# An offline list scheduler's model of the vector, scalar and GpSimd engines gets partition-quadrant gaps, sum gaps and a shared-port rule

## The chip, the cores and the metric

The kernel runs on one core of one Trainium2 chip. The metric is the device time of one execution in microseconds (us). The core's engines are called by the names of the profile: PE (TensorE, matrix products; PEld its weight loads), DVE (VectorE), ACT (ScalarE), POOL (GpSimd) and SP (SyncE, which issues the DMAs). Each engine works through its own list of instructions strictly in the order in which the program wrote them, and waits at semaphores for results of the others.

## The reference

One sequence of 512 tokens, width 1024, float32 throughout. Two layers of mLSTM beside sliding-window attention, with a squared-ReLU MLP; then one block of three attentions (called NSA below):

```python
for l in range(2):
    h = rmsnorm(x, norm_mix_g[l])
    proj = h @ w_in[l]                    # mLSTM q,k,v,o and gates; attention q,k,v; two branch gates
    hm = mlstm(silu(causal_conv(mqk)), mv, igate, fgate)          # 4 heads
    hm = headnorm(hm) * g * sigmoid(mo)
    ha = sliding_window_attention(aq, ak, av, sinks, rel_bias)    # 16 heads, window 128
    x = x + (sigmoid(ga) * (hm @ w_branch_m) + sigmoid(gb) * (ha @ w_branch_a)) @ w_out[l]
    h = rmsnorm(x, norm_mlp_g[l])
    x = x + square(relu(h @ w_up[l])) @ w_down[l]                 # 1024 -> 4096 -> 1024
x = rmsnorm(x, final_norm_g)
q, kv, g, z = split(rms_norm(x, gain) @ w_in2)
kc, vc = compress_kv(k_c), compress_kv(v_c)      # blocks of 32 keys, stride 16, a small MLP
o = sigmoid(g) * [attend(q,kc,vc), attend_selected(q,k_s,v_s), attend_window(q,k_w,v_w)] * silu(z)
out = x + o.sum(branches) @ w_out2
```

With 512 tokens the selected blocks are all blocks, so that branch is full causal attention.

## The kernel before

Every large product is a `gemm` of 128x128 stationary tiles with 128x512 moving tiles. Both operands are split into a high and a low part of a shorter float format, and `mm3` adds three products (high x high, high x low, low x high). Weights come from memory in tiles `raw` of 128x1024 or less; ACT writes their high part `wh`, and DVE or POOL their low part `wl` (`raw` minus `wh`). `xgh` and `xgl` are the two parts of the normalised activations. PSUM results of gemms are tiles `g` (four buffers, the same four also hold `gt`, the token-major products); attention scores are `S`, transposed probabilities `PT`, their parts `ph` and `pl`, head outputs `O`. In the attention, DVE adds bias and takes a maximum (`L`, `mn`), ACT takes the exponential with its row sum (`L`, `den`), `rd` is the reciprocal of the sum, ACT and DVE scale `L` by it, PE transposes it into `PT`, ACT and DVE split that, and PE multiplies by `v`. In the mLSTM part, `sums` and `bc` are small matmuls for norms and broadcasts, `ST` the products with the state. `cf` and `Z` belong to the compression of keys in NSA: `cf` is a scaled gemm result, and 32 small DVE operations `Z<-cf` write the overlapping blocks with the position added.

Nothing is issued while the program is built. The class `Recorder` takes each operation with its operands, works out which earlier operations it has to wait for, and `issue(RESERVE, WINDOW)` then runs a list scheduler over the whole program: it keeps a clock for each engine, always takes the operation that can start first by its model (for ties the one that is earliest in the program), at most 500 operations ahead of the oldest one not yet done, and hands out buffers. On PE, `pick` prefers an operation whose weights are loaded by the time the previous matmul ends. When all is ordered, one loop calls `op.fn(*op.args, **op.kw)`, so every instruction of the trace carries the same line (L320 before the change). The times in the model decide the order and nothing else.

The model before: `cost` gives the length of each operation; `LAT` the delay from an end on one engine to a start on another; `OVERLAP` a fixed amount by which the next operation of ACT, DVE or POOL starts ahead of the end of the last (100, 78, 38 ns); an operation with an `accum_out` (a sum along with its result) costs ACT 190 ns and DVE 150 ns more. `port` marks DVE operations with two inputs from SBUF, and POOL's: while one engine's such operation runs, the other engine's are not chosen, and an operation without the mark goes ahead of them.

## Time and profile before

| quantity | value |
| --- | --- |
| time of three runs | median 2189.2 us (2188.83 to 2190.84) |
| the profiled execution's own time | 2191.76 us |
| its span, first to last instruction | 2190.0 us |
| mean granted TensorE clock | 0.997 of full speed |
| PE busy | 2143.8 us, 98% of the span |
| DVE busy | 1383.5 us, 63% |
| ACT busy | 1065.0 us, 49% |
| POOL busy | 444.2 us, 20% |

The profile is of one execution; its time lies 1.76 us above its span, which is what starting and ending take outside the first and last instruction, and 2.6 us above the median of the three runs. "Busy" counts the time in which an engine has an instruction under way; the matmul ends are modelled, so a busy PE shows that it waits for nobody, not that each matmul is as fast as can be.

### The profile page before, as it was taken

The page shows a single profiled execution, that of the slowest core. Times are in us where ns is not written, and L with a number is a line of the kernel's source. Part 1 is how long each engine was busy: PE and PEld are TensorE (multiplying, and loading weights), DVE is VectorE, ACT ScalarE, POOL GpSimd, SP SyncE. Part 2 cuts the span into 40 slices and gives each one's busy share as a digit, 9 for nine tenths or more (in the row PEclk, how much of TensorE's full clock was granted, in tenths as well). Part 3 has the DMA queues.
Part 4 walks back from the last instruction along what each step waited for, and adds up shares of the span by engine and source line. Part 5 has one row for each costly group of instructions (what it writes and reads, how often), then busy time and mean ns, then how long its engine had stood idle before and what let it go on. Part 6 is the DMA issues. An engine that isn't in the chain of part 4 may idle for free.

```text
span 2190.0 us, 28079 instructions
## 1 busy us (share of the span) xinstructions
PE 2143.8 (98%) x10389; PEld 1773.4 (81%) x10389; DVE 1383.5 (63%) x2591; ACT 1065.0 (49%) x2066; POOL 444.2 (20%) x502
## 2 busy tenths in 40 slices
PE   8999999999999999999999999999999899999988
PEld 6787788888888888887777888888888798888777
DVE  7688995444343445678897445434435777888786
ACT  4466773234232334456675223323324356787783
POOL 2133551002000002014454002000001604232211
PEclk9999999999999999999999999999999999999999
DMA  5223222433333333322322333333333253222221
GB/s 159 81 66 90 81 73 88 134 96 95 98 96 96 97 97 116 97 78 76 97 68 77 120 111 97 96 96 97 97 100 116 85 167 97 68 65 67 92 93 43
DMA packets 72426, 206.10 MB, mean 94 GB/s; under 512 B 9761, under 2 KB 18593, under 8 KB 72289
## 3 DMA queue, kind: packets, MB, share of 16 engines
q1 hardware_dynamic: 72288, 204.31, 30.3%
q8 instruction: 81, 1.33, 0.2%
q14 instruction: 57, 0.46, 0.1%
HBM read 197.86 MB, written 6.42 MB: 93 GB/s over the span
## 4 chain that ended last, share of the span: by engine, by line
PE 43%; DVE 6%; ACT 2%; issue 2%; POOL 1%; POOLq 0%; DVEq 0%; ACTq 0%
PE g L320 34%; PE O L320 2%; PE PT L320 2%; PE S L320 2%; PE go L320 2%; DVE L L320 1%; PE gt L320 1%; DVE hal L320 1%; DVE wl L320 1%; PE hid L320 1%; POOL vb L320 0%; DVE Z L320 0%; ACT L L320 0%; DVE q L320 0%; ACT wh L320 0%
## 5 line engine op out<-in xcount | busy, mean ns | idle before, releaser
L320 ACT ACTIVATE wh<-raw 128x1024 fp32r<-128x1024 f32 (+2 forms) x344 | 355.5, 1034 | 784.6 <-PE g L320 590.8
L320 PE MATMUL g<-xgl,wh 128*128 128x512 f32 x1512 | 596.1, 394 | 2.5 <-DVE xgl L320 2.5
L320 PE MATMUL g<-xgh,wl 128*128 128x512 f32 x1512 | 594.8, 393 | 3.3 <-POOL wl L320 3.3
L320 PE MATMUL g<-xgh,wh 128*128 128x512 f32 x1512 | 595.4, 394 | 1.7 <-ACT xgh L320 1.5
L320 DVE TENSOR_TENSOR wl<-raw,wh 128x1024 fp32r<-128x1024 f32 (+2 forms) x327 | 410.9, 1257 | 125.4 <-ACT wh L320 124.4
L320 PEld LDWEIGHTS g<-xgh,wl 128*128 128x128 f32 x1512 | 284.9, 188 | 60.1 <-POOL wl L320 5.0
L320 PEld LDWEIGHTS g<-xgl,wh 128*128 128x128 f32 x1512 | 284.7, 188 | 59.7 <-DVE xgl L320 5.0
L320 PEld LDWEIGHTS g<-xgh,wh 128*128 128x128 f32 x1512 | 285.1, 189 | 56.5 <-ACT xgh L320 2.2
L320 POOL TENSOR_TENSOR sq<-sq 128x512 f32<-128x512 f32 x50 | 80.5, 1609 | 596.1 <-ACT sq L320 586.3
L320 PE MATMUL g<-hidh,wh 128*128 128x512 f32 x512 | 199.2, 389 | 0.0
L320 PE MATMUL g<-hidh,wl 128*128 128x512 f32 x512 | 199.2, 389 | 0.0
L320 PE MATMUL g<-hidl,wh 128*128 128x512 f32 x512 | 199.2, 389 | 0.0
L320 DVE TENSOR_TENSOR x<-x,g 128x512 f32<-128x512 f32 x80 | 55.0, 687 | 204.5 <-PE g L320 204.5
L320 ACT ACTIVATE L<-L,mn 128x256 f32<-128x256 f32 (+3 forms) x256 | 131.4, 514 | 38.8 <-DVE mn L320 35.7
L320 DVE SCALAR_TENSOR_TENSOR hz<-g,Rb 128x512 f32<-128x512 f32 x64 | 44.3, 692 | 157.8 <-PE g L320 152.3
L320 PEld LDWEIGHTS g<-hidh,wl 128*128 128x128 f32 x512 | 96.1, 188 | 20.0
L320 PEld LDWEIGHTS g<-hidh,wh 128*128 128x128 f32 x512 | 96.1, 188 | 20.0
L320 PEld LDWEIGHTS g<-hidl,wh 128*128 128x128 f32 x512 | 96.1, 188 | 19.8
L320 DVE TENSOR_TENSOR pl<-PT,ph 128x512 fp32r<-128x512 f32 (+1 forms) x160 | 79.8, 526 | 27.8 <-ACT ph L320 26.4
L320 PE MATMUL gt<-wh,xgh 128*128 128x512 f32 (+3 forms) x256 | 88.5, 347 | 5.0 <-DVE cf L320 5.0
L320 PE MATMUL gt<-wl,xgh 128*128 128x512 f32 (+3 forms) x256 | 88.5, 347 | 2.2 <-DVE wl L320 2.2
L320 PE MATMUL gt<-wh,xgl 128*128 128x512 f32 (+3 forms) x256 | 88.6, 346 | 0.0
(308 smaller groups left out, 3734.2 us busy)
## 6 DMA issues: line engine op xcount, KB each, us to landing
raw<-wf SPq DMA_DIRECT2D x258, 512.0 KB, 3.5
raw<-wn SPq DMA_DIRECT2D x41, 512.0 KB, 3.8
raw<-wmv SPq DMA_DIRECT2D x16, 512.0 KB, 3.6
x<-x SPq DMA_DIRECT2D x16, 256.0 KB, 4.2
bt<-E SPq DMA_DIRECT2D x16, 256.0 KB, 5.0
xsp<-x SPq DMA_DIRECT2D x16, 256.0 KB, 2.0
raw<-w SPq DMA_DIRECT2D x8, 512.0 KB, 3.8
bn<-E SPq DMA_DIRECT2D x16, 256.0 KB, 4.3
```

The source lines that it names most:

```text
L320: op.fn(*op.args, **op.kw)
```

## The change

No operation is added, removed or resized; each engine has the same instructions before and after, in another order. The diff replaces the numbers and a rule in the scheduler's model:

```diff
-OVERLAP = {PE: 0, ACT: 100, DVE: 78, POOL: 38, SP: 0}
+GAP = {ACT: (-95, 24, -2, 116), DVE: (-82, 31, -75, 40), POOL: (-38, 43, -38, 43)}
+ACC = {ACT: 93, DVE: 9}
+PORT = {DVE: 143, POOL: 116}
...
-            return 200 + 0.84 * n - (22 if _psum(ins[0]) else 0) + 88 * min(scalars, 2), False
+            return 192 + 0.842 * n - (22 if _psum(wide[0]) else 0) + 88 * min(scalars, 2), False
...
+            if name == "tensor_tensor_scan":
+                return 1209, both
+            if name in ("tensor_copy", "tensor_scalar") and not _psum(wide[0]):
+                return 150 + n / 1.92 + 60 * scalars, n > 4
+            return 148 + 1.05 * n + 60 * scalars, both
...
-            op.occ += 100 if eng == ACT else 60
-            op.cost += 190 if eng == ACT else 150
...
+        def gap(op):
+            e = op.eng
+            if e not in GAP:
+                return 0.0
+            held = wq[e].get(op.writes[0], op.writes[1]) != op.writes[1] or \
+                any(rq[e].get(m, x) != x for m, x in op.reads)
+            return GAP[e][2 * after[e] + held]
...
-                held = max(f, port[DVE if e == POOL else POOL]) if e in (DVE, POOL) else f
-                for k, s in ((0, f), (1, held)):
-                    if ready[e][k]:
-                        c = (s, ready[e][k][0], e, k)
-                        if best is None or c[0] < best[0] or c[0] == best[0] and c[2] == best[2] and c[1] < best[1]:
-                            best = c
...
+                lim = f + (GAP[e][0] if e in GAP else 0)
+                while pending[e] and pending[e][0][0] <= lim:
+                    heappush(ready[e], heappop(pending[e])[1])
+                if ready[e]:
+                    s = lim
+                elif pending[e]:
+                    s = pending[e][0][0]
...
-                op.start, op.end = t, t + op.cost
-                free[e] = t + op.occ
-                if op.port:
-                    port[e] = op.end - 60
+                t = max(t, free[e] + gap(op))
+                op.start, f = t, t + op.cost
+                if op.port:
+                    h = hold[POOL if e == DVE else DVE]
+                    if h > t:
+                        f = max(f, h + op.cost - PORT[e])
+                    hold[e] = f
+                free[e], after[e] = f, op.acc
+                op.end = f + (ACC[e] if op.acc else 0)
```

How far the order moves: of PE's instructions two thirds keep their place, of DVE's and ACT's about half; the furthest on PE goes 79 places, on DVE 36, on ACT 20, on POOL 5, on SP 3. The MLPs and the products with `w_branch` and `w_out` (about 360 to 840 us and 1200 to 1700 us of the trace) are unmoved. Three places follow.

**The start, DVE.** `sq` are squares for the norm, `xgl` the low parts of the activations, `oh` one-hot tables for the bias, `wl_151` the low part of the weight that the first token-major product `gt` needs. Before:

```order
SCALAR_TENSOR_TENSOR xgl_97<-x_95,pc_74,xgh_96 128x512
TENSOR_TENSOR sq_112<-x_98 128x512
SCALAR_TENSOR_TENSOR xgl_100<-x_98,pc_74,xgh_99 128x512
...
CAST oh_174<-oh_173 64x512
CAST oh_179<-oh_178 64x512
CAST oh_183<-oh_182 64x512
TENSOR_TENSOR selh_125<-ident_115 36x512
TENSOR_TENSOR wl_151<-raw_149,wh_150 128x528
```

After:

```order
SCALAR_TENSOR_TENSOR xgl_97<-x_95,pc_74,xgh_96 128x512
SCALAR_TENSOR_TENSOR xgl_100<-x_98,pc_74,xgh_99 128x512
...
TENSOR_TENSOR sq_112<-x_98 128x512
...
TENSOR_TENSOR wl_151<-raw_149,wh_150 128x528
TENSOR_TENSOR wl_154<-raw_152,wh_153 128x528
TENSOR_TENSOR wl_157<-raw_155,wh_156 128x528
...
CAST oh_174<-oh_173 64x512
```

The four casts `oh` go behind `wl_151`, `wl_154` and `wl_157`, and `sq_112` behind the last `xgl`.

**Attention of layer 1, near 253 us, PE.** `g_673` is a gemm that ends there, `g_711` the next one, `PT` and `O` the attention of one group of heads. Before:

```order
MATMUL g_673<-xgl_106,wh_671 128x512
MATMUL PT_648<-ident_115,L_636 128x128 x2
MATMUL PT_651<-ident_115,L_638 128x128 x2
MATMUL g_711<-xgh_81,wh_709 128x512
MATMUL g_711<-xgh_81,wl_710 128x512
MATMUL g_711<-xgl_82,wh_709 128x512
MATMUL g_711<-xgh_87,wh_709 128x512
MATMUL O_647<-ph_649,v_138 128x256
```

After:

```order
MATMUL g_673<-xgl_106,wh_671 128x512
MATMUL g_711<-xgh_81,wh_709 128x512
...
MATMUL g_711<-xgl_91,wh_709 128x512
MATMUL PT_648<-ident_115,L_636 128x128 x2
MATMUL PT_651<-ident_115,L_638 128x128 x2
MATMUL g_711<-xgh_93,wh_709 128x512
MATMUL g_711<-xgh_93,wl_710 128x512
MATMUL g_711<-xgl_94,wh_709 128x512
MATMUL O_647<-ph_649,v_138 128x256
```

Nine matmuls of `g_711` now stand ahead of the first `PT`.

**The start of NSA, near 1736 to 1754 us, DVE.** `cf_2886` and `cf_2891` empty the two PSUM buffers that the products `gt` still lack; `wl_2905` is the low part of the weight that these products read next. Before (23 more `Z` between the fourth row and the fifth, 8 behind the last):

```order
TENSOR_TENSOR cf_2872<-g_2876,Rb_2855 128x512
TENSOR_TENSOR cf_2877<-g_2881,Rb_2855 128x512
TENSOR_TENSOR cf_2886<-g_2890,Rb_2855 128x512
TENSOR_TENSOR Z_2868<-cf_2872,pc_74 64x4x31
...
TENSOR_TENSOR cf_2891<-g_2895,Rb_2855 128x512
TENSOR_TENSOR wl_2905<-raw_2903,wh_2904 128x608
```

After (15 more `Z` behind the third row, 15 more behind the sixth):

```order
TENSOR_TENSOR cf_2872<-g_2876,Rb_2855 128x512
TENSOR_TENSOR cf_2877<-g_2881,Rb_2855 128x512
TENSOR_TENSOR Z_2868<-cf_2872,pc_74 64x4x31
...
TENSOR_TENSOR cf_2886<-g_2890,Rb_2855 128x512
TENSOR_TENSOR cf_2891<-g_2895,Rb_2855 128x512
TENSOR_TENSOR Z_2882<-cf_2886,pc_74 64x4x31
...
TENSOR_TENSOR wl_2905<-raw_2903,wh_2904 128x608
```

`cf_2891` has 16 `Z` ahead of it instead of 24, and `wl_2905` all 32 instead of 24. On PE the four tiles of `gt` were filled side by side before; now the first two go on through their next weight tiles before the other two begin, and the four matmuls that read `wl_2905` first come behind 16 others that wait for `cf_2886` and `cf_2891`. Before, the wait for `cf_2891` had 26 matmuls up to and with the last of these four behind it.

## Rows read from the trace of the kernel before

**Rows 1.** The page, section 1: busy time of each engine.

```profile
PE 2143.8 (98%) x10389; PEld 1773.4 (81%) x10389; DVE 1383.5 (63%) x2591; ACT 1065.0 (49%) x2066; POOL 444.2 (20%) x502
```

**Rows 2.** Stretches: length, busy us (instructions) of PE, PEld, DVE, ACT, POOL; clock; DMA.

```profile
0.00:60.00 60.00, 51.46 (x241) 39.52 (x242) 43.20 (x80) 28.28 (x47) 14.47 (x22) 0.97 0.49 153
60.00:360.00 300.00, 292.13 (x1467) 238.19 (x1465) 246.25 (x547) 188.12 (x436) 112.53 (x134) 1.00 0.26 77
360.00:900.00 540.00, 540.00 (x2435) 448.25 (x2434) 249.85 (x290) 178.67 (x230) 35.48 (x24) 1.00 0.34 105
900.00:1200.00 300.00, 292.18 (x1468) 238.06 (x1467) 244.35 (x552) 187.52 (x435) 111.30 (x133) 1.00 0.26 78
...
1680.00:1800.00 120.00, 113.75 (x595) 97.44 (x594) 86.89 (x127) 62.15 (x97) 45.16 (x60) 0.99 0.39 125
1800.00:2040.00 240.00, 239.47 (x1346) 203.67 (x1344) 193.44 (x497) 176.52 (x414) 75.15 (x86) 1.00 0.27 81
2040.00:2190.00 150.00, 134.86 (x726) 111.18 (x726) 111.41 (x276) 92.55 (x222) 26.70 (x28) 0.97 0.22 71
```

**Rows 3.** PE's waits over the whole span: total us, times, longest us.

```profile
PE PT L320 <- ACT L L320: 11.2, 15, 1.8
PE gt L320 <- DVE cf L320: 5.0, 1, 5.0
PE g L320 <- POOL wl L320: 3.3, 4, 1.3
PE gt L320 <- DVE wl L320: 2.2, 1, 2.2
PE sums L320 <- ACT sqh L320: 2.1, 3, 1.2
PE ST L320 <- DVE w L320: 2.1, 2, 1.0
PE ptc L320 <- DVE Lc L320: 1.9, 1, 1.9
```

**Rows 4.** DVE, timeline at the start: start, us, operation, idle before.

```profile
17.04 1.77 DVE L320 TENSOR_TENSOR sq<-x 128x512 f32<-128x512 f32 x1
...
23.62 2.17 DVE L320 CAST oh<-oh 64x512 fp32r<-64x512 f32 x3
...
26.32 0.69 DVE L320 TENSOR_TENSOR wl<-raw,wh 128x528 fp32r<-128x528 f32 x1
```

**Rows 5.** POOL, timeline at the start.

```profile
14.90 3.36 POOL L320 TENSOR_TENSOR sq<-sq 128x512 f32<-128x512 f32 x2 [1.29 <-ACT sq L320]
```

**Rows 6.** PE, timeline near 250 us.

```profile
249.68 0.39 PE L320 MATMUL g<-xgh,wl 128*128 128x512 f32 x1
...
252.63 0.39 PE L320 MATMUL g<-xgl,wh 128*128 128x512 f32 x1
253.99 0.73 PE L320 MATMUL PT<-ident,L 128*128 128x128 f32 x4 [0.98 <-ACT L L320]
```

**Rows 7.** PE's waits from 240 to 360 us.

```profile
PE PT L320 <- ACT L L320: 4.3, 6, 1.0
```

**Rows 8.** PE's waits from 1080 to 1200 us.

```profile
PE PT L320 <- ACT L L320: 4.7, 7, 1.0
```

**Rows 9.** DVE, timeline of the start of NSA.

```profile
1735.38 1.29 DVE L320 TENSOR_TENSOR cf<-g,Rb 128x512 f32<-128x512 f32 x2 [1.44 <-ACT Rb L320]
...
1737.44 10.42 DVE L320 TENSOR_TENSOR Z<-cf,pc 64x124 f32<-64x124 f32 x24
```

**Rows 10.** PE, timeline of the start of NSA.

```profile
1748.64 0.52 PE L320 MATMUL gt<-wh,xgh 128*128 128x304 f32 x1 [5.02 <-DVE cf L320]
...
1752.23 0.30 PE L320 MATMUL gt<-wh,xgh 128*128 128x304 f32 x1
...
1753.74 0.30 PE L320 MATMUL gt<-wl,xgh 128*128 128x304 f32 x1
```

**Rows 11.** A stretch behind that wait, columns as in rows 2.

```profile
1749.00:1752.00 3.00, 3.00 (x14) 3.00 (x14) 2.99 (x7) 0.00 (x0) 2.94 (x7) 0.50 0.56 173
```

## The prediction

> **What bounds the kernel now.** I read the busy times first: PE is busy for 2143.8 of 2190.0 us [rows 1]. The next engine, DVE, has 63%. So no engine but PE is full, and the change, which adds and removes nothing, can only act through the 46 us in which PE stands still. The table by stretches says where they lie [rows 2]: 8.5 us in the first 60; 7.9 and 7.8 in the mLSTM and attention of the two layers (60 to 360 and 900 to 1200 us); 6.2 at the start of NSA; 0.5 from 1800 to 2040; 15.1 from 2040 on, of which a part follows the last matmul. In 360 to 900 PE is busy for the whole 540.00 us; there the order is unmoved, and nothing can come or go. The list of PE's waits says for whom [rows 3]: transposes `PT` for ACT's scaled `L` 11.2 us, `gt` for one `cf` 5.0, gemms for a POOL-made `wl` 3.3, `gt` for `wl` at the start 2.2, and three of about 2 us. This is the stock from which any gain comes; the gemm itself costs 0.227 us for each matmul (13 steps from 249.68 to 252.63) [rows 6] and stays.

> The sums below are made against the profiled execution's own 2191.8 us; the median of the runs is 2.6 us lower, and I take that off at the end.

> **Start.** DVE works without a pause up to `wl_151`, for which PE waits 2.2 us [rows 3]. Three casts `oh` of together 2.17 us stand right ahead of it and its `selh` [rows 4] and go behind; their results are first read by PE in the bias products, behind all of these `gt`, in the new order too. So `wl_151` comes about 2.1 us sooner, and with it everything behind: **-2.1**. `sq_112` also moves. It took 1.77 us, while a comparable operation alone takes 0.69, because it met POOL's additions, 14.90 to 18.26 us [rows 4, 5]. Bounds: -3.2 if it no longer meets them (1.1 more), -1.0 if another operation meets them in its place. Waits ahead of this one (for `xgl`) are in series with `wl_151` and not counted again.

> **Attention of the two layers.** PE waits 4.3 us in six places and 4.7 in seven for `L` [rows 7, 8], 0.7 us each. At the place shown the wait is 0.98 [rows 6]; the new order puts nine gemm matmuls there, 9 x 0.227 = 2.0 us of work that is ready. Elsewhere I count 5 to 10 such matmuls, late in the phase more. The gemm runs out of matmuls no earlier in sum, since the same ones were done later; what may come back is a wait at the last `O`, whose results the branch product needs, but the next gemms still lie between. I take 80% of 9.0: **-7.2**. Bounds: all (-9.0), or -2.0 where ACT, which is idle ahead of its own scaling as well, makes `L` late by as much again.

> **mLSTM.** Two waits `ST` for DVE's `w`, together 2.1 us [rows 3]: the operation `nMd` that the exponential ahead of `w` reads moves ahead of two splits `kl` on DVE. I take **-2.0** (bounds -2.1 and 0). Against it, the first `sums` matmul stands 17 places earlier on PE, that is 17 x 0.227 = 3.9 us, while the ACT operation `sqh` that it waits for stands only 3 to 10 places earlier; that wait is about 0.5 us now in each layer (`sums`: 2.1 us in three, the longest 1.2 in NSA) [rows 3], and I let each grow by 0.5: **+1.0** (bounds 0 and +2.4, when `sqh` gains 2.6 of the 3.9). `bc` goes five places back, 1.1 us of cover for a wait of 0.4 in each layer: **-0.7** (0 to -0.8).

> **Start of NSA.** Here the change puts a new wait in the place of one that it removes. 24 `Z` take 10.42 us, 0.434 each [rows 9]. Before: PE waits 5.0 us for `cf_2891`, goes on at 1748.64, and starts the first four matmuls that read `wl_2905` until 1753.74, the 26th from there [rows 10]. After: the first two `cf` end near 1737.1 (1735.38 + 1.29, and some 0.5 later, since the norm's `sums` and `bc` move back), 16 `Z` at 0.434 to 1744.1, two `cf` (1.29) to 1745.4, 16 `Z` to 1752.3, `wl_2905` (0.7 as `wl_151` [rows 4]) near 1753.1. PE waits about 2 us for the `cf`, does 16 matmuls, and waits again some 5 for `wl_2905`; of the 26 only four are left then, the last at 1753.1 + 3 x 0.14 = 1753.5. [...] So -0.2 + 1.5: **+1.3**. Bounds -0.2 (no slow stretch) and +1.6. Behind it, `wl_2918` comes later by eight `zl` that DVE does first; they fill pauses of DVE ahead of it, so I take nothing, with the bound +1 inside the range.

> **NSA from 1800 us.** Up to 2040 there is half a microsecond to gain [rows 2]. The attention moves forward by 9 to 27 places on PE against the gemms; DVE's reciprocal and ACT's scaling move forward as well, so that I expect few waits: **+1.0** (0 to +5). From 2040 on lie most of the 3.3 us of waits for POOL's `wl` and the 1.9 for `Lc` (`ptc`) [rows 3]; in the new order attention matmuls stand where the first `wl` is late, and the scores that `Lc` is made from come some ten matmuls (2.3 us) earlier, with two more DVE operations of 0.7 in their way. I take **-3.0** (bounds -7 and +3). DMA issues move by at most three places on SP, and no wait of PE in rows 3 ends with a DMA; nothing for these.

> **Sum.** -2.1 - 7.2 - 2.0 + 1.0 - 0.7 + 1.3 + 1.0 - 3.0 = -11.7; 2191.8 - 11.7 = 2180.1 for a profiled run, and 2177.5 for the median.

> **A rule that speaks against the change.** `sq_112` took 1.77 us beside POOL, and its end, 18.81, lies 0.55 behind that of POOL's additions, 18.26 [rows 4, 5]: it seems to have stood until the port came free. [...]

> **Rivals.** *The waits only move* (within 0.2%, that is 4.4 us): the layers' attention gives the low bound, -2.0, and `sums` takes +2.4, while start, `ST` and `bc` (-4.8), NSA's +1.3 and +5 and no gain at the end follow: +1.9, 2191 us. For it: 0.7 us is short, and the same engines feed the next matmul. Against it: nine ready matmuls for 0.98 us is twice what is missing. I let it stand for all sums from -4.4 to +4.4, at its middle 2189. *DVE stands in POOL's holds* (slower): the model no longer keeps such operations apart. POOL has 134 operations in each layer's stretch [rows 2]; an operation that meets one loses about 1.1 us (1.77 against 0.69) [rows 4]. If 17 more in each layer do, DVE is 37 us later in sum; if half of that reaches PE, which waits for DVE's results in order, that is +18, and 2191.8 - 11.7 + 18 - 2.6 = 2195.5. It decides from about 30 such meetings on; below 20 it is hidden. For it: DVE is busy for 246 of 300 us there. Against it: such meetings happen in the present order too, for the old rule only looked at a port taken when it chose. *More is recovered*: all of the first bounds together, -3.2 - 9.0 - 2.1 - 0.8 - 0.2 - 7 = -22.3, 2167 us.

> **How the numbers follow.** The forecast of some -6 to -17 us has 0.58, more than that 0.10, the waits that only move 0.18, the port 0.14. So faster by over 0.2% (under 2184.8) has 0.68, same 0.18, slower 0.14. 0.2% is about what a measurement of this kernel can tell from no change. The range from 2167 to 2191 leaves out the port and little more; it takes in the waits that only move. The forecast's own range is 2172 to 2183.

> **What the profile after would show.** Right: `PT` for `L` falls from 11.2 to 3 us or less, `ST` for `w` is gone, `gt` for `wl` at the start is followed by the same matmuls 2 us sooner, and near 1750 there are two waits of PE, of about 2 and 5 us, the second on `wl`, with a granted clock of 0.5 behind it. Both layers' stretches are 4 to 5 us shorter. Wrong: many DVE operations of 1.8 us where 0.7 was, with PE waiting for DVE; `sums` or `sc` waits over 1.5 us in a layer; PE waits in NSA between 1800 and 2040.

## The result and the profile after

The changed kernel takes 2165.06 us (median of four runs, 2163.57 to 2165.97), the kernel before, run beside it, 2189.93 (2188.83 to 2190.84): 24.9 us less, a ratio of 0.9886 with a 95% interval of 0.9869 to 0.9903. I had forecast 2177.5, some 12 us less, and a range down to 2167. The sign was right, the size is twice the forecast, and the result lies 2 us below the range. The profiled execution took 2164.52 us with a span of 2162.7, 27.3 below the span of before.

The page of the kernel after, busy times:

```profile
PE 2134.9 (99%) x10389; PEld 1780.6 (82%) x10389; DVE 1375.4 (64%) x2591; ACT 1063.7 (49%) x2066; POOL 439.9 (20%) x502
```

Against [rows 1] PE is busy for 8.9 us less with the same instructions, and it stands idle for 27.8 us in place of 46.2, 18.4 less; together these are the 27.3. That busy time can fall says that "busy" is no fixed amount of work. The stretches after, with the columns of [rows 2]:

```profile
0.00:60.00 60.00, 52.78 (x246) 41.37 (x247) 40.93 (x81) 29.00 (x48) 16.43 (x22) 0.97 0.50 156
60.00:360.00 300.00, 300.00 (x1519) 249.80 (x1518) 246.22 (x552) 190.59 (x439) 108.76 (x134) 1.00 0.28 82
...
900.00:1200.00 300.00, 300.00 (x1516) 250.22 (x1516) 244.27 (x547) 189.75 (x437) 110.04 (x135) 1.00 0.28 82
...
1680.00:1800.00 120.00, 111.22 (x627) 97.40 (x625) 83.97 (x146) 56.29 (x91) 47.54 (x87) 0.97 0.40 121
1800.00:2040.00 240.00, 238.85 (x1345) 204.54 (x1344) 203.92 (x520) 188.90 (x447) 70.05 (x59) 1.00 0.26 77
```

From 60 to 360 us PE's busy time rose from 292.1 to the full 300.0 us, 7.9 more; but the matmuls in brackets rose from 1467 to 1519. At 0.227 us a matmul, 52 more are 11.8 us of work. Read the count beside the time: it is the count that the end follows. PE's waits over the whole span after, columns as in [rows 3]:

```profile
PE gt L346 <- DVE wl L346: 6.3, 1, 6.3
PE sums L346 <- ACT sqh L346: 3.9, 1, 3.9
PE warm L346 <- ACT z L346: 2.3, 1, 2.3
PE gt L346 <- DVE cf L346: 2.3, 1, 2.3
PE g L346 <- POOL wl L346: 2.0, 2, 1.6
PE O L346 <- DVE pl L346: 1.2, 3, 0.8
```

`PT` for `L` (11.2 us before) and `ST` for `w` (2.1) are gone; between 60 and 1200 us the list has no wait of PE at all. Two long ones are new: `sums` at the start, `gt` for `wl` at the start of NSA.

For this kernel and those below I cut the span at the start of certain matmuls that stand at the same work in every order (such as the first `gt_208` that reads `wl_223`, or the first `g_619` that reads `wl_618`). Lengths in us of the profiled executions, up to the last matmul:

| kernel | start | mLSTM 1 | attention + MLP 1 | mLSTM 2 | attention + MLP 2 | start of NSA | rest of NSA |
| --- | --- | --- | --- | --- | --- | --- | --- |
| before | 66.5 | 163.2 | 676.8 | 165.1 | 651.1 | 39.6 | 421.3 |
| after | 65.4 | 159.2 | 668.3 | 161.2 | 642.5 | 41.8 | 417.6 |
| old port rule | 64.1 | 161.5 | 668.8 | 162.9 | 643.4 | 39.9 | 425.7 |
| no quadrant gap | 63.3 | 160.2 | 676.2 | 162.2 | 650.4 | 41.3 | 418.1 |
| none on DVE | 63.9 | 160.2 | 675.9 | 162.2 | 650.0 | 41.9 | 416.7 |
| none on ACT | 64.7 | 159.0 | 670.4 | 161.4 | 644.1 | 42.0 | 418.3 |
| old price of sums | 63.9 | 159.1 | 668.4 | 161.0 | 642.7 | 41.8 | 431.1 |
| older latencies | 65.3 | 159.2 | 668.4 | 161.2 | 642.6 | 42.0 | 414.2 |
| before + quadrant gap | 65.5 | 161.3 | 669.1 | 163.2 | 643.4 | 39.4 | 424.5 |
| last version | 63.9 | 159.2 | 668.4 | 161.2 | 642.6 | 32.8 | 417.7 |

Of the 27.3 us, 17.0 come from the attention of the two layers (8.4 and 8.6), 7.8 from their mLSTM, 1.1 from the start and 3.6 from the rest of NSA; the start of NSA lost 2.2. These differences are of unrounded lengths, and a tenth can differ from the table's.

### The profile page after: what moved, and what is told of

Same layout as the page of the kernel before. It is cut to its first block, busy times and chain, and to the rows that moved or that the text cites. A ratio compares the mean times of both kernels' runs of the same rounds, so it can differ in the third digit from the quotient of the medians.

```text
span 2162.7 us, 28087 instructions
## 1 busy us (share of the span) xinstructions
PE 2134.9 (99%) x10389; PEld 1780.6 (82%) x10389; DVE 1375.4 (64%) x2591; ACT 1063.7 (49%) x2066; POOL 439.9 (20%) x502
## 4 chain that ended last, share of the span: by engine, by line
PE 95%; DVE 2%; POOL 1%; issue 1%; ACT 1%; DMA 0%; SPq 0%; DVEq 0%; POOLq 0%; ACTq 0%
PE g L346 75%; PE gt L346 6%; PE S L346 3%; PE O L346 3%; PE PT L346 2%; PE num L346 1%; PE go L346 1%; PE ST L346 1%; DVE Z L346 1%; POOL vb L346 0%; PE bc L346 0%; PE hid L346 0%; POOL sq L346 0%; PE sums L346 0%; DMA x<-x 0%
## 5 line engine op out<-in xcount | busy, mean ns | idle before, releaser
L346 DVE TENSOR_TENSOR pl<-PT,ph 128x512 fp32r<-128x512 f32 (+1 forms) x160 | 78.9, 525 | 23.3 <-ACT ph L346 22.5
```

## The experiments

Each result is the median of the runs with the lowest and the highest, and then the ratio to the kernel before, run beside it, with its 95% interval in square brackets. Code is shown in extracts; `...` stands for what is left out.

### What each part of the model carries

**Port rule undone.** The changed kernel, but an operation that uses the port is again held back while the other engine has it, and the marks are the old ones.

```diff
-                if ready[e]:
-                    s = lim
...
+                held = max(lim, hold[DVE if e == POOL else POOL] - 60) if e in (DVE, POOL) else lim
+                for k, s in ((False, lim), (True, held)):
+                    mine = [j for j in ready[e] if ops[j].port == k]
...
```

> The changed model with the old port rule: port operations of DVE and POOL are kept apart again, all else new. If the port rule is what freed PE from its waits in the two layers, each layer's stretch gets its 7.5 us of idle back and the time goes to about 2180 to 2190 us. If the gaps and the sums did it, the time stays within 5 us of the changed kernel's 2165. At the start the squares are then kept away from POOL's additions as before, so the wait of 3.9 us for the norm's sums goes and one for a weight's low part of about 2 us comes back, in either case.

Measured 2174.70 us (2173.51 to 2175.63), 0.9929 [0.9906, 0.9951] of before, 9.6 above the changed kernel, which lies between my two forecasts. The attention stays within 0.9 us of the kernel after; the mLSTM gives back 2.3 and 1.7 us of its 4.0 and 3.9, NSA 8.1 behind its start, while the start and the start of NSA are 1.3 and 1.9 shorter. At the start the wait for `sums` is gone and one of 2.2 us for `wl` is back, as expected. The model's port rule, which I feared, is a gain in the mLSTM; what it is worth in NSA the control below leaves open.

**Quadrant gap undone**, on all engines.

```diff
-            return GAP[e][2 * after[e] + held]
+            return GAP[e][2 * after[e]]
```

> The changed model without the gap at a change of partition quadrant: every next operation starts early, as in the old model; sums, port and costs stay new. If the quadrant gap (0.11 us on DVE, 0.12 on ACT, at most some 60 operations in an attention step) carries the gain, PE's waits for the transposes come back and the time goes above 2175 us. If not, it stays at 2160 to 2170.

Measured 2182.21 (2180.05 to 2182.92), 0.9963 [0.9947, 0.9979], 17.1 above the changed kernel. Both layers' attention is back at the length of before, the mLSTM gives back 1.0 each. A line of PE's waits over the whole span of this kernel:

```profile
PE PT L346 <- ACT L L346: 4.7, 10, 1.2
```

Only 4.7 us of these waits are back, 3.5 of them (nine) in the layers, where the waits of all kinds come to 6.7; the two attention stretches are 15.8 us longer than after. A stretch can lose far more than its waits show; I come to that below.

**Price of sums undone.**

```diff
-GAP = {ACT: (-95, 24, -2, 116), DVE: (-82, 31, -75, 40), POOL: (-38, 43, -38, 43)}
-ACC = {ACT: 93, DVE: 9}
+GAP = {ACT: (-95, 24, 5, 124), DVE: (-82, 31, -22, 91), POOL: (-38, 43, -38, 43)}
+ACC = {ACT: 190, DVE: 150}
```

> The changed model with the old price of a sum: its result 190 ns (ACT) or 150 ns (DVE) late instead of 93 and 9, and the engine held as long as before. The exponentials and maxima of the attention all make sums. If that price put the attention in the wrong place, PE waits for the transposes again and the time goes above 2175 us; if not, 2160 to 2170.

Measured 2177.83 (2176.34 to 2178.83), 0.9943 [0.9921, 0.9966], 12.8 above the changed kernel. The time is above the 2175 that I named, but not for the reason that I gave with it: the layers don't change and have no wait for the transposes. The rest of NSA is 13.4 us longer, the start 1.5 shorter.

Undone one at a time, the three parts cost 9.6, 17.1 and 12.8 us, together 39.5, more than the 24.9 of the whole change: they can't be added up.

**A control: the older latencies alone.** The change also replaces four values of `LAT`, the delays between engines, by 1 or 2 ns, which the list of the change does not name; this run puts the old ones back.

```diff
-LAT = {(PE, ACT): 204, (PE, DVE): 200, (PE, POOL): 240, (ACT, PE): 53, (ACT, ACT): 32, (ACT, DVE): 33, (ACT, POOL): 78,
-       (ACT, SP): 26, (DVE, PE): 55, (DVE, ACT): 34, (DVE, DVE): 34, (DVE, POOL): 80, (DVE, SP): 28, (POOL, PE): 54,
+LAT = {(PE, ACT): 202, (PE, DVE): 200, (PE, POOL): 240, (ACT, PE): 53, (ACT, ACT): 32, (ACT, DVE): 33, (ACT, POOL): 79,
+       (ACT, SP): 27, (DVE, PE): 55, (DVE, ACT): 34, (DVE, DVE): 34, (DVE, POOL): 79, (DVE, SP): 28, (POOL, PE): 54,
```

> A control: only the table of delays between engines is the old one, four numbers that differ by 1 or 2 ns; 7% of PE's instructions change places. What an arbitrary small reshuffle is worth: 2162 to 2168 us, with the two layers' stretches still free of waits. If it moves by more than 5 us, single runs of the other three say little about their rule.

Measured 2161.87 (2161.25 to 2162.49), 0.9874 [0.9845, 0.9902]: 3.2 us below the changed kernel, all of it in the rest of NSA, the layers equal to 0.1 us. So in NSA a change of 2 ns that means nothing shuffles the order and is worth 3 us; differences of that size there say nothing about a rule.

**Quadrant gap undone on DVE alone**, and then **on ACT alone**.

```diff
-            return GAP[e][2 * after[e] + held]
+            return GAP[e][2 * after[e] + (held and e != DVE)]
```

> The changed kernel, with the quadrant gap switched off in the model of DVE alone. With the gap off everywhere the attention stretches of the two layers had grown from 113.0 and 119.2 us to 120.9 and 127.1. Theory A (what is mispriced is DVE's work on scores and masks, whose pieces change quadrant from one to the next): attention stretches of 118 to 121 and 124 to 127 us, transposes waiting for L again, 2178 to 2184 us. Theory B (it is ACT's row of exponentials and scalings of L): attention stretches stay within 1.5 us of 113 and 119, and the time within 2160 to 2170. Both in part: 115 to 118 and 121 to 124.

> The changed kernel, with the quadrant gap switched off in the model of ACT alone. Theory A (DVE's gap carries the attention gain): stretches stay within 1.5 us of 113 and 119, 2160 to 2170 us. Theory B (ACT's does): stretches of 118 to 121 and 124 to 127 us, transposes waiting for L some 4.7 us in each layer, 2176 to 2184 us. I hold B the likelier, since the wait that vanished was one for ACT's L.

Without it on DVE 2179.81 (2179.07 to 2180.86), 0.9957 [0.9941, 0.9973]; on ACT 2167.93 (2167.62 to 2168.23), 0.9902 [0.9882, 0.9922]. Theory A holds, but for ACT's stretch in layer 1, which I had allowed 1.5 us: without DVE's gap the attention of the layers loses 7.6 and 7.5 us, without ACT's 2.0 and 1.5, without any 7.9 and 7.8. I had held B the likelier, because the wait that went was one for ACT's `L`: the engine named in that wait was the last in a chain, and by these losses most of the delay came from the engine ahead of it.

**The quadrant gap alone, added to the kernel before.**

```diff
+        more = {ACT: 119, DVE: 113, POOL: 81}
...
+                if wq[e].get(op.writes[0], op.writes[1]) != op.writes[1] or any(rq[e].get(m, x) != x for m, x in op.reads):
+                    t = max(t, free[e] + more.get(e, 0))
...
```

> The kernel before, its model kept, with one thing added: a gap in front of an operation that changes quadrant (ACT 119 ns, DVE 113 ns, POOL 81 ns more). Theory (the quadrant gap alone carries the attention gain): attention stretches fall from 121.1 and 127.5 us to 113 to 115 and 119 to 121, those of the mLSTM stay near 163 and 165, and the time is 2170 to 2176 us. Rival (the gap helps only along with the new prices of sums and of the port, since the old overlaps are wrong in other places too): attention stretches 118 or more and 124 or more, 2182 to 2192 us.

Measured 2174.93 (2174.87 to 2174.98), 0.9934 [0.9914, 0.9954], 14.5 below the kernel before. The theory holds in the time and in the attention: with the MLP it is 7.7 us shorter in each layer (the cut at its end lies 2 us earlier, so the attention alone reads as 111.4 and 117.7). The mLSTM, which I expected unchanged, is 1.8 and 1.9 shorter. The gap alone in the mLSTM and the port rule there (2.3 and 1.7) together come near its 4.0 and 3.9.

The timeline of DVE in the kernel after, inside the attention, shows the two gaps themselves:

```profile
257.62 0.41 DVE L346 TENSOR_TENSOR hal<-O,hah 64x256 fp32r<-64x256 f32 x1
257.96 0.47 DVE L346 CUSTOM_DVE_ANT_0 L<-S,bt,nsink 128x256 f32<-128x256 f32 x1
258.36 0.08 DVE L346 DVE_READ_ACCUMULATOR2_ANT mn<- 128x1 f32 x1
258.46 0.42 DVE L346 TENSOR_TENSOR hal<-O,hal 64x256 fp32r<-64x256 f32 x1
258.92 0.48 DVE L346 CUSTOM_DVE_ANT_0 L<-S,bt,nsink 128x256 f32<-128x256 f32 x1
```

The first `L` starts 0.07 us ahead of the end of the `hal` before it (257.62 + 0.41 = 258.03); the second, behind another `hal` of 64 partitions, 0.04 behind its end (258.46 + 0.42 = 258.88). In the attention of layer 1 before, the trace has some 100 gaps of DVE of the second kind, +0.034 on the mean, and some 130 of the first, -0.08 (reads of an accumulator left out of these). Some 70 of the 100 stand behind an operation without a sum. The old model gave these -0.078, so by this count its DVE ran 70 x 0.113 = 7.9 us ahead of the chip over that stretch; behind a sum, where it let the engine go 0.06 later, it was off by about half as much. That it therefore put PE's `PT` where the model's `L` was ready and the chip's was not is my reading; the runs show that the gap moves the attention's time. They switched the gap in the model, and did not vary the partitions by themselves.

### What a wait costs

**Six, and then twelve, small copies on ACT ahead of 32 scalings of `L`** in the two layers, with the order of the changed kernel otherwise kept: extra work that makes `L` late.

```diff
+            if id(op) in slow:
+                for _ in range(6):
+                    self.scalar.real.activation(self.scr[0], self.scr[1], AF.Copy)
...
```

> The changed kernel with six extra copies of 128x112 on ACT (about 0.2 us each, 1.2 in all, into a tile that nothing reads) ahead of the scaling of L in each of the 32 half steps of the layers' attention; the order is untouched. It shows the cover that the changed order has: with more than 1.2 us of it the layers' stretches stay as they are and the time stays within 3 us; with less, waits of PE for L appear.

> The same with twelve copies, about 2.4 us. PE has to wait in many places now. If a wait costs PE just the idle time that the list of waits shows, the layers' stretches grow by that idle time. If it costs more, because the matmul behind it can't overlap the tail of the one ahead and the next comes late too, they grow by about 0.25 to 0.3 us more for each wait; with some 30 waits that is 8 to 9 us on top.

With six 2216.13 us (2216.12 to 2216.15), 1.0118 of before; with twelve 2300.63 (2299.21 to 2302.04), 1.0504. PE's waits over the whole span with six:

```profile
PE O L351 <- ACT ph L351: 20.1, 17, 1.6
PE PT L351 <- ACT L L351: 19.3, 18, 1.5
```

A copy took 0.29 us, six of them 1.8 where I had 1.2, and the order does not cover that in 35 places. The kernel lost 2216.1 - 2165.1 = 51.1 us and shows 39.4 us of such waits: on the mean each cost its idle time and 0.33 us more, with the late starts that show no idle time counted in. With twelve it lost 135.6 for 88.6 us of waits (34 of them), 1.4 more each; there the mean granted clock also fell (0.969 over the span in place of 0.994 with six, and 0.92 from 60 to 370 us), so that this run can't price the wait alone.

Where such a surplus comes from can be read at one place, where it is 0.27. In [rows 6] the last gemm before the wait starts at 252.63 and `PT` at 253.99. What follows there in the kernel before (timeline of PE):

```profile
254.48 0.48 PE L320 MATMUL g<-xgh,wh 128*128 128x512 f32 x1
254.79 0.40 PE L320 MATMUL g<-xgh,wl 128*128 128x512 f32 x1
```

And the same three steps in the kernel after, where nothing is waited for:

```profile
248.49 0.40 PE L346 MATMUL g<-xgl,wh 128*128 128x512 f32 x1
248.72 0.60 PE L346 MATMUL PT<-ident,L 128*128 128x128 f32 x4
249.08 0.47 PE L346 MATMUL g<-xgh,wh 128*128 128x512 f32 x1
249.40 0.39 PE L346 MATMUL g<-xgh,wl 128*128 128x512 f32 x1
```

Before: 254.79 - 252.63 = 2.16 us; after: 249.40 - 248.49 = 0.91. The wait shown as 0.98 cost 1.25, 0.27 more. A gemm matmul counts as busy for 0.39 us though the next starts 0.227 behind it; of a late start the first 0.16 us lie under that tail and are not shown as idle, and the step behind the wait is 0.13 longer (0.49 against 0.36). The 0.39 is a modelled end, and so the 0.16 (0.39 less 0.227) is an estimate; the starts are measured.

This can be counted for a whole stretch, as start-to-start steps beyond the usual one (the median step of the same two shapes in the kernels before and after, 60 to 1690 us). In the attention of layer 1 before, 12 steps are late by over 0.1 us, 7.2 us in all (8 of them show as waits, 5.3 us); after, none. Without the quadrant gap 23 are, 6.4 us in all, of which the stretch shows 3.0 as idle. Many short late starts weigh like a few long ones and hardly show. With all steps that are late by over 0.02 us, the two attentions come to 20.4 us before and 4.1 after, the two mLSTM to 13.4 and 6.2. The difference, 23.5 us, is nearly all of what the layers gained (24.8), and the trace of before shows only 15.1 us of idle time in these four stretches.

### The two new waits

**Both moved by hand**: the norm's `sums` at the start behind `gt` matmuls that are ready, and `wl_2905` right behind `cf_2891` on DVE; then the same with the older latencies.

```diff
+        w = next(op for op in dve if self.name(op).startswith("wl_2905"))
+        dve.remove(w)
+        n = [i for i, op in enumerate(dve) if self.name(op).startswith("cf_2891")][-1]
+        dve.insert(n + 1, w)
...
```

> The changed order with two places moved by hand, all else in its place. On DVE wl_2905 goes right behind cf_2891, ahead of 16 Z; on PE the norm's sums, sc and bc at the start go behind those products gt that are ready. The first should take away the wait of 6.3 us for wl_2905 and the slow matmuls behind it, 6 to 8 us in all; the second the wait of 3.9 us for the sums, and slow matmuls behind it, 3 to 5 us. Together 2152 to 2157 us. If what follows only waits for Rb (start) or for the 16 Z and the compression (NSA) in its turn, most of it comes back later.

> The control with the old table of delays (2161.9 us) and the same two places moved by hand. If the two moves are worth what the waits cost and nothing else depends on them, it is as much faster than 2161.9 as the kernel without the old table is than 2165: 2149 to 2154 us.

Measured 2159.56 (2159.26 to 2160.85), 0.9861 [0.9846, 0.9876], and 2157.30 (2156.27 to 2158.79), 0.9852 [0.9835, 0.9868], both some 3 us slower than the ranges that I gave. In the first kernel the start gains 1.4 us, the start of NSA 1.9; there the wait of 6.3 became one of 4.4, for `wl_2908`, the next weight, which still stood behind 16 `Z`:

```profile
PE gt L347 <- DVE wl L347: 4.4, 1, 4.4
```

**The last version**: as the second of these, and at the start of NSA `cf_2886` behind 8 `Z`, `cf_2891` behind 14, `wl_2905` and `wl_2908` behind the first 16, `wl_2911` behind five more; DVE's later `zl` and ACT's `zh`, parts of the operands of `hid`, were moved along with these.

```diff
+        n = find(dve, "cf_2877", True) + 1
+        dve[n + 8:n + 8] = c86
+        dve[n + 15:n + 15] = c91
+        dve[n + 18:n + 18] = w5 + w8
+        dve[n + 25:n + 25] = w11
...
```

> The changed kernel with the older table of latencies between engines (2161.9 us measured), the norm's sums at the start behind gt matmuls that are ready, and at the start of NSA on DVE and ACT cf_2886 behind 8 Z, cf_2891 behind 14, the weights wl_2905 and wl_2908 behind the first 16 Z, wl_2911 behind 5 more. Theory (the wait for wl there is one of order alone): PE's waits of gt for wl go, one for cf of 1 to 2 us stays, the stretch at the start of NSA falls from 41.8 us to 37 or less, and the time is 2152 to 2156 us. Rival (DVE is busy there without a pause from 1708 to 1737 us, so its work is what ends last): the wait passes to a later operand of DVE (hid, zl), the stretch stays at 38 to 40, and the time is 2156 to 2160 us, as with the simpler move (2157.3).

Measured 2153.20 (2152.61 to 2154.15), 0.9834 [0.9817, 0.9850] of before, inside the theory's range. The start of NSA takes 32.8 us in place of 41.8. Between 1690 and 1760 us the wait of `gt` for `wl` is gone and these are PE's waits; the stretch from 1690 to 1730 us runs at the full clock (second fence, columns as in [rows 2]):

```profile
PE g L347 <- DVE wl L347: 1.7, 1, 1.7
PE gt L347 <- DVE cf L347: 1.0, 1, 1.0
PE hid L347 <- DVE wl L347: 0.8, 1, 0.8
PE hid L347 <- DVE zl L347: 0.4, 1, 0.4
```

```profile
1690.00:1730.00 40.00, 37.76 (x206) 32.33 (x204) 30.58 (x56) 16.01 (x25) 27.33 (x49) 1.00 0.23 76
```

The rival is right in part: `hid` and one `g` now wait for DVE, 2.9 us in all, just behind the cut that ends the stretch. Against the control, which has the same latencies, the start of NSA gains 9.2 us, the rest of NSA loses 3.5 again, and 5.7 are left.

## Why the prediction was wrong in size

**The stock: the step that failed.** I wrote that the change "can only act through the 46 us in which PE stands still" and took the waits for "the stock from which any gain comes". In the layers that stock is 7.9 and 7.8 us [rows 2], and they gave back 24.8 (with the MLPs behind them): PE's busy time was no floor, but held late starts as well. A late matmul cost its idle time and about 0.3 us more (0.33 on the mean with six copies, 0.27 at the one place), and by the estimate above one that is late by less than 0.16 shows no idle time; at 0.33 the 23 waits that the trace of before names there would have been priced 15.7 + 23 x 0.33 = 23.3 us. The count of late steps gives 33.8 us before and 10.3 after.

**Attention: -7.2 forecast, -17.0 measured.** Place and mechanism were right: at the place shown nine gemms stand ahead of `PT`, and the wait is gone. Two sizes were off: not 80% but all of the waits went, and the late starts were worth more than the waits showed (20.4 us before, 4.1 after, against 9.0 of waits for `L`). That ACT would make `L` late again (the low bound, -2.0) didn't come; the experiments put the delay on DVE.

**mLSTM: -2.0 + 1.0 - 0.7 = -1.7 forecast, -7.8 measured.** `ST` went as said. `sums` didn't grow in the layers, against what I let it do, and the late starts counted for more here too (13.4 us before, 6.2 after, against 4.5 of idle time). Half of the gain is the port rule's (2.3 and 1.7 us), which I had only as a danger.

**Start: -2.1 forecast, -1.1 measured**, by two larger parts that nearly cancel, so that the forecast came near by luck. PE in the kernel before, then PE and POOL in the kernel after:

```profile
27.07 0.51 PE L320 MATMUL gt<-wl,xgh 128*128 128x264 f32 x2 [2.24 <-DVE wl L320]
```

```profile
22.38 0.51 PE L346 MATMUL gt<-wl,xgh 128*128 128x264 f32 x2
...
28.09 0.47 PE L346 MATMUL sums<-sqh,ones2r 128*2 128x512 f32 x1 [3.87 <-ACT sqh L346]
```

```profile
20.44 4.26 POOL L346 TENSOR_TENSOR sq<-sq 128x512 f32<-128x512 f32 x1 [2.63 <-DVE sq L346]
24.78 2.60 POOL L346 TENSOR_TENSOR sq<-sq 128x512 f32<-128x512 f32 x2
```

The `gt` for `wl_151` starts 4.7 us sooner. The casts were only part of that: of five squares and `xgl` that took DVE some 1.77 us before, three are left after, and the others take 0.7. Then 3.9 are lost right behind at `sums`: its squares are added up by POOL until 27.38. The growth of a `sums` wait that I looked for in the layers stood here.

**Start of NSA: +1.3 forecast, +2.2 measured**; the mechanism was right. I foresaw two waits of about 2 and 5 us and a granted clock of 0.5 behind the second; PE, then DVE, then a stretch behind the second wait:

```profile
1719.28 0.41 PE L346 MATMUL gt<-wh,xgh 128*128 128x304 f32 x1 [2.26 <-DVE cf L346]
...
1728.03 1.38 PE L346 MATMUL gt<-wl,xgh 128*128 128x304 f32 x4 [6.26 <-DVE wl L346]
```

```profile
1719.73 7.42 DVE L346 TENSOR_TENSOR Z<-cf,pc 64x124 f32<-64x124 f32 x16
1727.18 2.20 DVE L346 TENSOR_TENSOR wl<-raw,wh 128x608 fp32r<-128x608 f32 x3
```

```profile
1728.30:1732.00 3.70, 3.70 (x17) 3.70 (x18) 3.70 (x7) 0.02 (x1) 2.54 (x6) 0.57 0.75 255
```

The waits are 2.3 and 6.3; 16 `Z` took 7.42 us where I had 16 x 0.434 = 6.9. The granted clock of the stretch behind the wait was 0.57 on the mean: 0.50 from 1728.3 to 1731.4 us, as in [rows 11], and 1.00 from 1731.6 on. No run shows by itself the +1.5 that this forecast holds for slow matmuls; in its place the trace after shows 13 steps in 3.46 us behind the second wait (1728.03 to 1731.49), 1.7 more than 13 of the steps ahead of both waits (14 in 1.93 us from 1714.64, 0.138 each, clock 1.00).

**Rest of NSA: -2.0 forecast, -3.6 measured.** The control, worth -3.4 there by itself, shows that no forecast of this size had a ground; that mine came near is luck.

**The rivals.** That the waits only move is false for the layers, where none is left, and true for the start and the start of NSA. That DVE stands in POOL's holds is false in sum: DVE is busy for 8.1 us less than before and POOL for 4.3 less, and the old rule costs 9.6 us. The rival with more recovered came nearest; its bound, all waits at the idle time shown, was still too small.

What stays open is why the price of sums and the port rule are worth 13.4 and 8.1 us in NSA: they shuffle the order there, and a shuffle without meaning made 3.

## What to carry to other kernels

Price a wait of TensorE by the start-to-start steps around it, not by the idle time shown, and compare instruction counts of equal stretches instead of busy shares: here PE's waits cost some 0.3 us each beyond what they showed (0.33 on the mean of 35, 0.27 at one place). Where a planner's order leaves many short waits for one engine, compare the model's gaps with the trace's on the engine ahead of it in the chain: 0.11 us too little, a hundred times in a layer's attention, was worth some 7.5 us. One place where 32 small operations stand ahead of a weight that PE needs next, reordered by hand, took 9.2 us off its stretch; 5.7 were left when the waits behind it were counted. Look past the end of a stretch before you price it.

## What was not expected of the hardware

Where DVE and POOL met at the start, either could be the one that stood. In the kernel after, DVE went with no wait from 20.2 to 23.56 us through five operations with two inputs, a copy and a multiplication by a scalar. POOL's addition beside them took 4.26 us and ended 1.14 behind DVE's last; such an addition took 1.67 in the kernel before, and the two right behind this one, with DVE idle, 1.26 each. In the run without ACT's quadrant gap, it was DVE that stood in the same place, in a copy of 1.31 us that takes 0.22 after (two timelines, this run and the kernel after):

```profile
20.34 1.31 DVE L346 COPY jrev<-ident 128x128 f32<-128x128 f32 x1
```

```profile
20.81 0.22 DVE L346 COPY jrev<-ident 128x128 f32<-128x128 f32 x1
```

POOL's addition ahead of that copy took 1.60 us. The next two, the first of them beside the DVE operations that follow, took 5.02 where two undisturbed ones took 2.60, so POOL stood in its turn:

```profile
19.96 1.60 POOL L346 TENSOR_TENSOR sq<-sq 128x512 f32<-128x512 f32 x1 [2.62 <-DVE sq L346]
```

```profile
21.64 5.02 POOL L346 TENSOR_TENSOR sq<-sq 128x512 f32<-128x512 f32 x2
```

Which engine stands, these runs show only for this place, in these two forms.
